# Two DMA lanes and new prices in the planner of a decoder trunk, and its decay stores on GpSimd

## The chip, the cores and the metric

One core of a Trainium2 chip. The metric is the device time of one execution in microseconds, as the median of several runs. TensorE does the matmuls, VectorE, ScalarE and GpSimd the work on elements, SyncE issues most of the DMAs; each engine executes its own instructions in the order in which they were written, and waits at an instruction until the semaphores that it needs are there.

## The reference

A decoder trunk of two layers over 1024 positions of width 1024, in float32. Each layer has a token mixer beside a cross-attention of 4 heads into 256 memory tokens, one combined input projection, one output projection over the concatenated heads, and a squared-ReLU MLP of width 4096; both sums go through a layer norm.

```python
for i in range(DEPTH):                       # 2
    if i % N_MIXERS == 0:
        mix, xq = gdn_mixer(x, ...)          # gated DeltaNet, 8 heads of 128
    else:
        mix, xq = s5_mixer(x, ...)           # 64 groups of 64 complex states
    cross = memory_attention(xq, mem, w_kv_mem[i])
    h = jnp.concatenate([mix, cross], axis=-1) @ w_o[i]
    x = layer_norm(DN_ALPHA * x + h, ln1_g[i], ln1_b[i])
    f = jnp.square(jax.nn.relu(x @ mlp_w1[i])) @ mlp_w2[i]
    x = layer_norm(DN_ALPHA * x + f, ln2_g[i], ln2_b[i])
```

In the DeltaNet each head keeps a state S; a chunk of positions is solved with a triangular inverse of a matrix that holds the products of the keys, times beta, times the decay between two positions:

```python
decay = jnp.where(causal, jnp.exp(jnp.where(causal, diff, 0.0)), 0.0)
a_strict = jnp.where(strict, jnp.einsum('bhnid,bhnjd->bhnij', kb, k) * decay, 0.0)
...
attn = jnp.einsum('bhid,bhjd->bhij', qi, ki) * deci
```

## The kernel before, in words

**Matmuls.** A float32 product is made of three matmuls in a format of fewer bits: both operands are split into a high part (a cast by ScalarE) and a low part (the difference, by VectorE), and `mm3` (L422 to L424) adds high·high, low·high and high·low in PSUM. Nearly all of TensorE's time goes there, in steps of 128 by 128 by 512. VectorE's line of such a split is L378, L587, L635 or L991, by what is split.

**The delta rule.** Layer 0 works by head and half of the sequence (a half-head: 512 positions, four tiles of 128). `gdn_keys_out` (L1250) makes for each half-head the decay matrix D (`decay`, L1236: L1241 and L1243), the squared norms of the keys, the scaled keys kd, D times the factors (L1275), and stores D in DRAM (`ded`, L1276, by ScalarE's queue). From the products of the keys (kk, L1282) and D comes NT (L1283); its diagonal blocks go out by four DMAs `ntd` of GpSimd (L1286) and the whole by one, `ntf` (L1287). `gdn_inverse` and `gdn_invert_tiles` read them back and make the inverse in small products (iv, tv, mz: L1403 to L1433; the matmul L1408). `gdn_queries_out` (L1436) turns the queries (qt, L1444), takes their norms on ScalarE (jk, L1446), and reads D back as Dq (L1450, SyncE). `gdn_recur` (L1534) runs over the tiles of a head: ks = S·k (L1554), R (L1556, VectorE), pe = inverse·R (L1560), e (L1562, ScalarE), po (L1557 and L1572), pS (L1566), the next S (L1569 or L1571, VectorE). Projections of the next head (wi, wz, with the convolution at L1218 to L1226) are the work that lies between.

**The S5 layer.** `s5_read` (L2093) adds to each half's output py a product with s5t (L2100) and one of r with H (L2101). H is a tile of 256 KB that GpSimd's queue loads from DRAM (L2035).

**What sets the order.** The code writes the steps down in some order, and at the end of `run` one call of `settle` (L63; called in L2418) puts the instructions of all five engines from the start of layer 0 on into an order of its own. It is a list scheduler: it keeps a model time for each engine, gives each instruction a cost from `price` (L305: busy time, time until the result is there, and for a DMA the time that its bytes take), knows the buffers of each pool, and takes again and again the instruction that can begin first. All DMAs share one server in the model (`served`): each begins to move when the one before has moved. TensorE's order follows the written one within a reach of 40 us, the others may run up to 70 us ahead of what is due. The order that it finds is nailed down by dependencies. So a price changes no instruction, and yet may move any of them.

**The end.** The last layer norm (`layer_norm` with `last`, L550 to L557) works on three pieces of a row of 1024: 512, 256, 256, as the last matmuls deliver them; each piece is scaled in one pass (L554), and a second pass (L556) is followed by the store of that piece.

## Time and profile before

| what | us |
|---|---|
| median of 3 runs | 2468.33 (2463.03 to 2469.39) |
| the profiled execution | 2469.93 |
| its span, first to last instruction | 2468.2 |
| TensorE busy (granted clock 0.998) | 2438.1 |
| VectorE, ScalarE, GpSimd busy | 1928.6, 1302.2, 411.1 |

A row of a timeline gives the start, the duration, engine, line, operation, output and inputs with shapes, the number of instructions in the row, and in brackets how long the engine stood idle before it and what ended that. A matmul is pipelined: its duration overlaps the next one's, and the step from start to start is what it costs. A row of the waits gives who waited for whom: total, times, longest. Names of buffers in the profile lack their numbers; in the order below they have them.

### The profile page before, as it was taken

What the parts mean: (1) busy time and instruction counts of PE and PEld (TensorE: products, weight loads), DVE (VectorE), ACT (ScalarE), POOL (GpSimd) and SP (SyncE); (2) the same over time, 40 slices, a digit from 0 to 9 for tenths busy, and PEclk for the clock granted to TensorE, in tenths of its full rate; (3) what the DMA queues carried; (4) which work ended last, traced back from release to release, by engine and by line L of the source; (5) the groups of instructions that cost most, each with busy time, mean ns of one, the idle gap of its engine ahead of it and who ended that gap; (6) DMA issues with size and microseconds to landing.
All of it is one profiled execution on the core that took longest, in us unless ns stands there. A gap on an engine that the chain in (4) does not pass through costs nothing.

```text
span 2468.2 us, 36630 instructions
## 1 busy us (share of the span) xinstructions
PE 2438.1 (99%) x12055; PEld 2024.0 (82%) x12055; DVE 1928.6 (78%) x3537; ACT 1302.2 (53%) x2779; POOL 411.1 (17%) x629
## 2 busy tenths in 40 slices
PE   9999999999999999999999999999999999999998
PEld 7888888888887887878888888888888888888887
DVE  8786878777779999897888767786688756676868
ACT  7665565555467576554444255464376555544442
POOL 1242333313001034111100133012010000000002
PEclk9999999999999999999999999999999999999999
DMA  6463555747955767787543499569746544666432
GB/s 228 112 178 115 137 164 137 221 131 214 319 198 201 281 223 241 252 289 235 175 152 123 149 273 314 161 226 326 259 138 226 185 152 157 247 190 225 120 120 82
DMA packets 326544, 485.88 MB, mean 197 GB/s; under 512 B 106273, under 2 KB 136945, under 8 KB 326353
## 3 DMA queue, kind: packets, MB, share of 16 engines
q1 hardware_dynamic: 299680, 427.90, 52.9%
q0 software_dynamic: 23936, 50.85, 7.1%
q10 hardware_dynamic: 2736, 4.79, 0.5%
q8 instruction: 95, 1.56, 0.3%
q14 instruction: 97, 0.79, 0.1%
HBM read 325.59 MB, written 157.78 MB: 196 GB/s over the span
## 4 chain that ended last, share of the span: by engine, by line
PE 74%; DVE 9%; issue 7%; DMA 5%; ACT 3%; POOL 2%; SPq 0%; DVEq 0%; ACTq 0%; POOLq 0%
PE q L422 7%; PE q L423 7%; PE q L424 7%; PE tm L423 3%; PE tm L424 3%; PE tm L422 3%; PE pA L422 3%; PE pA L423 3%; PE pA L424 3%; PE wi L422 2%; PE wi L423 2%; PE wi L424 2%; PE pC L422 2%; PE pC L423 2%; PE pC L424 2%
## 5 line engine op out<-in xcount | busy, mean ns | idle before, releaser
L423 PE MATMUL q<-wkl,hkh 128*128 128x512 f32 x784 | 305.7, 390 | 1.1 <-DVE wkl L991 1.1
L422 PE MATMUL q<-wkh,hkh 128*128 128x512 f32 x784 | 305.9, 390 | 0.0
L424 PE MATMUL q<-wkh,hkl 128*128 128x512 f32 x784 | 305.4, 389 | 0.0
L990 ACT CAST wkh<-wr 128x512 fp32r<-128x512 f32 x168 | 105.0, 625 | 243.7 <-PE q L423 238.2
L991 DVE TENSOR_TENSOR wkl<-wr,wkh 128x512 fp32r<-128x512 f32 x168 | 115.9, 690 | 110.2 <-issue 79.3
L423 PEld LDWEIGHTS q<-wkl,hkh 128*128 128x128 f32 x784 | 147.2, 188 | 32.2 <-DVE wkl L991 1.9
L422 PEld LDWEIGHTS q<-wkh,hkh 128*128 128x128 f32 x784 | 147.2, 188 | 31.5 <-ACT wkh L990 0.8
L424 PEld LDWEIGHTS q<-wkh,hkl 128*128 128x128 f32 x784 | 147.2, 188 | 30.5
L549 POOL TENSOR_TENSOR mv<-mv,mhalf 128x1 f32<-128x1 f32 x32 | 29.2, 911 | 844.0 <-DVE mv L543 563.0
L422 PE MATMUL wi<-xTh,wih 128*128 128x512 f32 x384 | 159.2, 415 | 0.3 <-ACT xTh L1097 0.2
L423 PE MATMUL wi<-xTl,wih 128*128 128x512 f32 x384 | 153.1, 399 | 0.9 <-DVE xTl L1098 0.9
L424 PE MATMUL wi<-xTh,wil 128*128 128x512 f32 x384 | 152.8, 398 | 0.0
L991 DVE TENSOR_TENSOR hkl<-hr,hkh 128x512 fp32r<-128x512 f32 x188 | 128.9, 686 | 0.0
L990 ACT CAST hkh<-hr 128x512 fp32r<-128x512 f32 x188 | 116.4, 619 | 0.0
L422 PE MATMUL tm<-so 128*128 128x512 f32 x280 | 110.2, 398 | 0.9 <-ACT so L1746 0.9
L1747 DVE TENSOR_TENSOR so<-or,so 128x1024 fp32r<-128x1024 f32 x70 | 84.5, 1222 | 28.4 <-ACT so L1746 28.1
L1746 ACT CAST so<-or 128x1024 fp32r<-128x1024 f32 x70 | 71.8, 1050 | 58.0 <-DMA or<-wod 40.3
L423 PE MATMUL tm<-so 128*128 128x512 f32 x224 | 87.5, 394 | 0.0
L424 PE MATMUL tm<-so 128*128 128x512 f32 x224 | 87.1, 392 | 0.0
L424 PEld LDWEIGHTS wi<-xTh,wil 128*128 128x128 f32 x384 | 72.3, 188 | 15.0 <-issue 0.8
L422 PEld LDWEIGHTS wi<-xTh,wih 128*128 128x128 f32 x384 | 72.5, 189 | 14.1 <-issue 1.4
L423 PEld LDWEIGHTS wi<-xTl,wih 128*128 128x128 f32 x384 | 72.6, 189 | 12.8 <-DVE xTl L1098 1.6
(626 smaller groups left out, 7256.3 us busy)
## 6 DMA issues: line engine op xcount, KB each, us to landing
hr<-hd SPq DMA_DIRECT2D x204, 256.0 KB, 2.7
wr<-in_w_dram SPq DMA_DIRECT2D x112, 256.0 KB, 5.2
hd<-u SPq DMA_DIRECT2D x92, 256.0 KB, 2.6
w1r<-in_w_dram SPq DMA_DIRECT2D x36, 512.0 KB, 3.6
hd<-hid SPq DMA_DIRECT2D x60, 256.0 KB, 2.3
hd<-p SPq DMA_DIRECT2D x60, 256.0 KB, 2.6
w1r<-in_w_dram SPq DMA_DIRECT2D x56, 256.0 KB, 4.0
wir<-in_w_in_dram SPq DMA_DIRECT2D x23, 512.0 KB, 4.1
```

The source lines that it names most:

```text
L422: mm(ps, a[0], b[0], start=start, stop=False, skip_group_check=onto)
L423: mm(ps, a[0], b[1], start=False, stop=False, skip_group_check=onto)
L424: mm(ps, a[1], b[0], start=False, stop=stop, skip_group_check=onto)
L549: nc.gpsimd.tensor_tensor(mv[:, 3:4], mv[:, 2:3], self.mhalf[:, 0:1], op=ALU.pow)
L990: nc.scalar.copy(hi, s)
L991: nc.vector.tensor_tensor(lo, s, f32(hi), op=ALU.subtract)
L1746: nc.scalar.copy(hi, r)
L1747: V.tensor_tensor(lo, r, f32(hi), op=ALU.subtract)
```

## The change

The change has four parts.

1. The planner's DMA model has two lanes: one for the queues of SyncE and ScalarE, one for GpSimd's. Each has its own server. Where both have work, the new method `carry` makes each slower by half of what overlaps. A lane holds at most eight transfers; the next waits for the eighth before it. What GpSimd issues takes 0.8 us more.
2. `price` has other numbers: for the issue of a DMA (ScalarE 0.3, the others 0.4, GpSimd by the number of pieces), for its latency, for large DMAs of GpSimd, for ScalarE's copies of fewer than 128 partitions and its accumulating reads, for GpSimd's smallest operation and VectorE's small ones.
3. The second pass of the last layer norm runs over two pieces of 512, so there are two stores and not three.
4. The store of D, one for each of the sixteen half-heads, is issued by GpSimd.

The instructions stay the same ones otherwise; lines of the changed kernel are 14 higher in most places.

```diff
-            free, locked, served, head, kind = {e: 0.0 for e in names}, 0.0, 0.0, 0, ""
+            lanes = [[], []]
+            free, locked, served, head, kind = {e: 0.0 for e in names}, 0.0, [0.0, 0.0], 0, ""
...
+                        if cost[x][2] and len(lanes[e == E.Pool]) >= 8:
+                            r = max(r, lanes[e == E.Pool][-8] + lag)
...
-                    served = max(served, r + length - moves) + moves
-                    length = served - r + late
+                    length = self.carry(served, e == E.Pool, r + length - moves, moves) - r + late + (0.8 if e == E.Pool else 0)
+                    lanes[e == E.Pool].append(r + length - late - (0.8 if e == E.Pool else 0))
...
+    def carry(self, served, q, at, moves):
+
+        t = max(served[q], at)
+        both = max(0.0, min(served[not q] - t, 2 * moves))
+        served[q] = t + moves + both / 2
+        served[not q] += both / 2
+        return served[q]
...
-            return (0.45 if i.engine != E.Pool else 0.6), 1.6 + size / 300 + (0.0 if k >= 512 else 0.7) + (2 if i.engine == E.Pool else 0.0), moves
+            issue = {E.Activation: 0.3, E.Pool: 0.5 + 0.36 * size / min(k, 2048) * (2 if size > 500 else 1)}.get(i.engine, 0.4)
+            return issue, 1.6 + size / 300 + (0.0 if k >= 512 else 0.4) + (1.2 if i.engine == E.Pool else 0.0), moves
...
-            t = 0.02 + 0.87e-3 * big if i.opcode == "Memset" else 0.5 if big < 2 else 1.0 if big < 8 else 0.17 + 2.1e-3 * big
+            t = 0.02 + 0.87e-3 * big if i.opcode == "Memset" else 0.95 if big < 2 else 1.0 if big < 8 else 0.17 + 2.1e-3 * big
...
-            for c in at:
+            for c in (slice(0, HALF), slice(HALF, 1024)):
                 nc.vector.scalar_tensor_tensor(y[:, c], y[:, c], mv[:, 3:4], gb[1][:, c], op0=ALU.mult, op1=ALU.add)
                 nc.sync.dma_start(last[0][:, c], y[:, c])
...
-        nc.scalar.dma_start(self.ded[h, hf], d)
+        nc.gpsimd.dma_start(self.ded[h, hf], d)
```

How this moves the instructions is shown at three places. The first is on ScalarE, where the decay matrix D_4610 of a half-head is stored while an inverse is made (iv, tv) and a tile of a recurrence ends (e). Before:

```order
L1562 COPY e_4882<-pe_4880 128x128 [waits PE_49]
L1446 ACTIVATE jk,scr_93<-qt_4823 128x128
L1276 DMA ded<-D_4610 128x512 [waits DMAHW0_49,DVE_49]
L1421 COPY tv_1959<-mz_1960 32x4x32 [waits DVE_49]
L1421 COPY tv_1959<-mz_1960 32x4x32
L1446 ACTIVATE jk,scr_93<-qt_4823 128x128 [waits Activation_49]
L1425 COPY iv_4767<-iv_4860 32x4x32 [waits DVE_49]
L1446 ACTIVATE jk,scr_93<-qt_4823 128x128 [waits Activation_49] x2
L1425 COPY iv_4768<-iv_4860 32x4x32 [waits DVE_49]
```

and after:

```order
L1435 COPY tv_1959<-mz_1960 32x4x32 [waits DVE_49]
L1435 COPY tv_1959<-mz_1960 32x4x32
L1439 COPY iv_4767<-iv_4860 32x4x32 [waits DVE_49,PE_49]
L1576 COPY e_4882<-pe_4880 128x128 [waits PE_49]
L1460 ACTIVATE jk,scr_93<-qt_4823 128x128 [waits Activation_49]
L1235 ACTIVATE vT_4651<-wi_4741,scr_93 128x512 [waits DVE_49]
L1439 COPY iv_4768<-iv_4860 32x4x32 [waits DVE_49]
```

The store is gone from ScalarE's row, the two copies tv and the first iv stand ahead of e, and the second iv stands behind one square jk and the evacuation vT. On GpSimd the store stands ahead of the four ntd stores of its half-head.

The second place is TensorE at the turning of a half-head's queries, qt_4713; R_4738 comes from ks_4736, and qT_4458 is the tile that qt turns. Before:

```order
L1282 MATMUL kk_4638<-kT_278 128x128 x4
L423 MATMUL wi_4741<-xTl_12_130,wih_4656 128x512
L424 MATMUL wi_4741<-xTh_11_129,wil_4657 128x512
L1560 MATMUL pe_4754<-R_4738,iv_3635 128x128
L422 MATMUL wi_4741<-xTh_11_129,wih_4656 128x512
L423 MATMUL wi_4741<-xTl_12_130,wih_4656 128x512
L424 MATMUL wi_4741<-xTh_11_129,wil_4657 128x512
L1557 MATMUL po_4735<-S_4682,gb_4173 128x128
L422 MATMUL wi_4741<-xTh_11_129,wih_4656 128x512
L423 MATMUL wi_4741<-xTl_12_130,wih_4656 128x512
L1444 MATMUL qt_4713<-ident,qT_4458 128x128 x4
```

and after:

```order
L1568 MATMUL ks_4736<-S_4682,kT_278 128x128
L1296 MATMUL kk_4638<-kT_278 128x128 x4
L1574 MATMUL pe_4754<-R_4738,iv_3635 128x128
L436 MATMUL wi_4741<-xTh_11_129,wih_4656 128x512
L437 MATMUL wi_4741<-xTl_12_130,wih_4656 128x512
L438 MATMUL wi_4741<-xTh_11_129,wil_4657 128x512
L436 MATMUL wi_4741<-xTh_11_129,wih_4656 128x512
L1458 MATMUL qt_4713<-ident,qT_4458 128x128 x4
```

Before, 20 rows stand between ks_4736 and qt; now only kk, pe and four matmuls of wi do, and po_4735 comes later. VectorE has, for the same instructions, before:

```order
L1571 SCALAR_TENSOR_TENSOR S_4682<-S_4577,scr_93,pS_4680 128x128
L1226 SCALAR_TENSOR_TENSOR qT_4458<-th_4516,qT_4458 128x512
L1268 TENSOR_TENSOR scr_93<-scr_93 128x4
L1223 SCALAR_TENSOR_TENSOR qT_4459<-cv_4460,scr_93,qT_4459 128x512
L1269 TENSOR_TENSOR scr_93<-scr_93 128x4
L1556 SCALAR_TENSOR_TENSOR R_4738<-ks_4736,scr_93,mix_1742 128x128
```

and after:

```order
L392 TENSOR_TENSOR wzl_4848<-wzr_4845,wzh_4847 128x1024
L1281 RECIPROCAL scr_93<-scr_93 128x4
L1570 SCALAR_TENSOR_TENSOR R_4738<-ks_4736,scr_93,mix_1742 128x128
L1282 TENSOR_TENSOR scr_93<-scr_93 128x4
L1289 TENSOR_TENSOR D_4521<-D_4521,scr_93 128x512
L1283 TENSOR_TENSOR scr_93<-scr_93 128x4
L1297 SCALAR_TENSOR_TENSOR NT_4550<-kk_4549,D_4521 128x512
L702 TENSOR_TENSOR ws_4316<-ws_4315,ws_4316 128x512
L1240 SCALAR_TENSOR_TENSOR qT_4458<-th_4516,qT_4458 128x512
```

The last step on qT_4458 stood ahead of R_4738, and now stands behind it, behind the product in D_4521, NT_4550 and a sum of weights (ws).

The third place is TensorE in the S5 read of the other layer, at the product with H. Before, with wq a projection of the cross-attention's queries:

```order
L2100 MATMUL py_15955<-s5t_14549 128x128
L422 MATMUL wq_16035<-xTh_2658_14185,wqh_16031 128x512
L423 MATMUL wq_16035<-xTl_2659_14186,wqh_16031 128x512
L424 MATMUL wq_16035<-xTh_2658_14185,wql_16032 128x512
L422 MATMUL wq_16035<-xTh_2658_14185,wqh_16031 128x512
L423 MATMUL wq_16035<-xTl_2659_14186,wqh_16031 128x512
L424 MATMUL wq_16035<-xTh_2658_14185,wql_16032 128x512
L2101 MATMUL py_15955<-r_15824,H_2929_15876 128x127
```

and after, the last rows ahead of the same product:

```order
L436 MATMUL wq_16035<-xTh_2658_14185,wqh_16031 128x512
L437 MATMUL wq_16035<-xTl_2659_14186,wqh_16031 128x512
L438 MATMUL wq_16035<-xTh_2658_14185,wql_16032 128x512
L436 MATMUL wq_16035<-xTh_2658_14185,wqh_16031 128x512
L437 MATMUL wq_16035<-xTl_2659_14186,wqh_16031 128x512
L438 MATMUL wq_16035<-xTh_2658_14185,wql_16032 128x512
L436 MATMUL wq_16035<-xTh_2658_14185,wqh_16031 128x512
L2115 MATMUL py_15955<-r_15824,H_2929_15876 128x127
L2114 MATMUL py_15955<-s5t_14549 128x128
```

Between the product with s5t and the one with H stand six matmuls of wq before, and sixteen now (the nine ahead of those shown are of the same three kinds).

## The prediction

> **What bounds the kernel now.** The page's head and its first part come first, because they tell how much there is to win.

> ```profile
> span 2468.2 us, 36630 instructions
> PE 2438.1 (99%) x12055; PEld 2024.0 (82%) x12055; DVE 1928.6 (78%) x3537; ACT 1302.2 (53%) x2779; POOL 411.1 (17%) x629
> ```

> TensorE is busy for all but 2468.2 − 2438.1 = 30.1 us. The change leaves the number of matmuls as it is, so only those 30.1 us can shrink, plus whatever new idle time the new order makes. Next is the view of TensorE's waits: line that waited, what it waited for, total, times, longest.

> ```profile
> PE py L2101 <- DMA H<-h1d: 3.1, 1, 3.1
> PE iv L1408 <- ACT iv L1425: 2.5, 2, 2.1
> PE ks L1554 <- DVE S L1569: 1.9, 2, 1.1
> PE pA L423 <- DVE xB L587: 1.2, 1, 1.2
> PE q L423 <- DVE wkl L991: 1.1, 2, 0.6
> PE z L1046 <- DVE z L1043: 1.1, 1, 1.1
> PE po L1557 <- ACT on L1585: 1.1, 2, 0.6
> ...
> PE pA L424 <- DVE a1l L635: 0.9, 1, 0.9
> ```

> No cause is large; the longest single wait is 3.1 us, 0.13% of the span. The row of z is the start of the program, ahead of the planned stretch, and the end is seen in the timeline of the last microseconds (first TensorE's last matmul, then two of VectorE's instructions of the last layer norm):

> ```profile
> 2458.11 0.28 PE L424 MATMUL tm<-w2h,hk 128*128 128x256 f32 x1
> 2462.37 0.75 DVE L556 SCALAR_TENSOR_TENSOR y<-y,mv,gb 128x512 f32<-128x512 f32 x1
> 2463.04 0.87 DVE L554 SCALAR_TENSOR_TENSOR y<-tm,mv,gb 128x256 f32<-128x256 f32 x2
> ```

> From 2458.4 to 2468.2 TensorE has ended: 9.8 us. So 30.1 − 1.1 − 9.8 = about 19 us is all that a better order could take out between start and end. The forecast is therefore a sum of small waits, each read as a race: how long TensorE has work from what releases a chain until it needs the chain's result (counted in the order), and how long the chain takes (from the rows).

> **Term 1, the load of H.** The timeline of TensorE at the longest wait:

> ```profile
> 1552.37 0.39 PE L423 MATMUL wq<-xTl,wqh 128*128 128x512 f32 x1
> 1552.59 0.40 PE L424 MATMUL wq<-xTh,wql 128*128 128x512 f32 x1
> 1556.12 0.77 PE L2101 MATMUL py<-r,H 128*128 128x127 f32 x2 [3.13 <-DMA H<-h1d]
> ```

> Two 128x512 matmuls start 0.22 us apart (0.227 over a longer stretch), though each is shown as 0.39 long. In the order given with the change, six such rows stand between the two py matmuls before and sixteen now; with what moved ahead of the first of them it is twelve more between the step that releases the load and the use of it. 12 × 0.227 = 2.7 of the 3.13 us: **−2.7**. If the load comes just as much later, the gain is nothing; if all of the wait goes, −3.1.

> **Term 2, the store that held ScalarE.** ScalarE's timeline around the second row of the waits, then two rows of the other engines there:

> ```profile
> 430.88 0.67 ACT L1221 ACTIVATE vT<-wi,scr 128x512 f32<-128x512 f32 x1
> 431.65 0.27 ACT L1562 COPY e<-pe 128x128 f32<-128x128 f32 x1
> 431.81 0.28 ACT L1446 ACTIVATE jk<-qt 128x128 bf16<-128x128 f32 x1
> 431.98 0.21 ACT L1446 ACTIVATION_READ_ACCUMULATOR jk<-qt 128x1 f32 x1
> 434.21 0.33 ACTq L1276 DMA_DIRECT2D ded<-D  x1
> 434.57 0.60 ACT L1421 COPY tv<-mz 32x128 f32<-32x128 f32 x2 [2.39 <-DMA bz<-ntf]
> ...
> 436.79 0.26 ACT L1425 COPY iv<-iv 32x128 f32<-32x128 f32 x1
> ```
> ```profile
> 431.00 0.69 DVE L1275 TENSOR_TENSOR D<-D,scr 128x512 f32<-128x512 f32 x1 [0.20 <-ACT D L1243]
> ...
> 437.10 1.10 PE L1408 MATMUL iv<-tv,na 128*128 128x64 f32 x8 [2.08 <-ACT iv L1425]
> ```

> D is ready at 431.69 and ScalarE is free at 432.19, but the store of D is issued at 434.21, and the row behind it names as releaser the DMA bz<-ntf, a load of SyncE. In the order, this store waits for VectorE and for a DMA completion count. So ScalarE's instructions behind it (tv, jk, iv) stood still for 2.02 us, and TensorE's wait for iv is 2.08. After the change no DMA is on ScalarE. What is late next is the chain from pe: e 0.27, one jk 0.38 (431.81 to 432.19), the new vT 0.67, iv 0.26, about 1.6 us and some latency, against nine 128x512 matmuls and one pS, over 2.0 us. I take the whole wait: **−2.1** (at worst −1.5).

> **What the sixteen stores cost GpSimd.** Rows of the tile's view, of GpSimd's lines, and of the DMA view (last column: us from issue to landing):

> ```profile
> L1276 ACTq DMA_DIRECT2D ded<-D x16: 326/326/353, 47.9 to 518.7; - x16
> L1450 SPq DMA_DIRECT2D Dq<-ded x16: 319/400/737, 174.8 to 599.3; - x16
> L1287 POOL DMA_DIRECT2D ntf<-NT x16 | 9.2, 574 | 1.1 <-DMA tv<-t 1.1
> ntf<-NT POOLq DMA_DIRECT2D x16, 256.0 KB, 3.6
> ded<-D ACTq DMA_DIRECT2D x16, 256.0 KB, 2.9
> ```

> ScalarE is freed of 16 × 0.326 = 5.2 us, on an engine that is busy for 53%: nothing by itself. GpSimd gets 16 × 0.574 = 9.2 us, on top of 17%: nothing either, as long as its queue is not late. Behind each moved store stand the four ntd stores and ntf of the same half-head, 0.57 us later where D and NT are ready at once; NT is one 0.65 to 0.69 us VectorE instruction later than D, which covers it. The store lands some 0.7 us later; the first and the last load of it follow 127 and 81 us behind: hidden. If a store were to wait for a count of GpSimd's own queue, ntd and with it the inverse would slip by as much as ScalarE did here, 2 us, once: in the range.

> [...]

> **Term 3, splits of VectorE.** Of the rows above, xB (1.2), wkl (1.1) and a1l (0.9) are TensorE waiting for the low part of an operand. In the new order seven 128x512 matmuls (1.6 us) stand at xB where its product followed at once, and likewise 0.9 to 3.6 us more at the others. All three go: **−3.2**.

> **Term 4, small ones.** Of ks (1.1 and 0.8) the new order adds 0.4 and 0.9 us of work between S and its use, so 1.2 goes; of po 0.3: **−1.5**.

> **Term 5, a new wait at qt.** Here the order moves the other way: qt now comes after ks, four kk, pe and four wi, while VectorE's last step of qT moved behind R. VectorE's rows there, and TensorE's for kk:

> ```profile
> 417.65 0.35 DVE L1556 SCALAR_TENSOR_TENSOR R<-ks,scr,mix 128x128 f32<-128x128 f32 x1
> ...
> 420.12 1.22 DVE L378 TENSOR_TENSOR wzl<-wzr,wzh 128x1024 fp32r<-128x1024 f32 x1
> 421.26 0.68 DVE L1275 TENSOR_TENSOR D<-D,scr 128x512 f32<-128x512 f32 x1
> 421.89 0.06 DVE L1214 MEMSET cv<- 128x3 f32 x1
> 421.98 0.69 DVE L1283 SCALAR_TENSOR_TENSOR NT<-kk,D 128x512 f32<-128x512 f32 x1
> ```
> ```profile
> 419.70 1.16 PE L1282 MATMUL kk<-kT 128*128 128x128 f32 x8
> ```

> From R on VectorE has R 0.35, D 0.68, NT 0.69, then a sum of ws and the step of qT of NT's size, 0.69 each, and small ones: 3.1 to 3.4. TensorE has kk 0.9 (1.16 less the overlap at its end), pe 0.1 and wi 0.9, about 2.0 to 2.2. That is +0.9 at least; with wzl's 1.22 between S and R not hidden, up to +2.6. I take **+2.0**, since wzl now stands right ahead of R and is near the upper end.

> **Term 6, less room elsewhere.** At seven places (evictions of on, so and hid by ScalarE, and r of the S5 read) the new order leaves 0.2 to 0.7 us less work than the chain took. The nearest price is po's row, 1.1 for two; I take half of that each, 7 × 0.3 = **+2.1** (0 to +4).

> **Term 7, what the order doesn't show.** Over 700 matmuls move by more than a microsecond, mostly away from any wait. I take **+1.5**, between −2 and +4.

> **The last layer norm.** One 512-wide instruction (0.75) in place of two 256-wide (0.87 together): −0.1, and the last store is 512 wide and not 256: +0.1 to +0.2. Nothing.

> Sum: −2.7 − 2.1 − 3.2 − 1.5 + 2.0 + 2.1 + 1.5 = −3.9. The profiled execution took 2469.93, 1.7 more than its span, and 1.6 more than the median 2468.33; so 2466.0 for it, and on the median **2464.4**. Differences below 0.3% (7.4 us) are about what a measurement of this kernel can't tell from no change.

> **The rivals.**
> A, the waits of before go and none come: the planner's prices are nearer to the trace, so terms 5 to 7 vanish, and some of the remaining 19 us goes too: −9.5 to −14, 2454.3 to 2458.8. For it: no row of before shows the new waits. Against: two of them are counted in the order.
> B, nothing net: a wait moves to the next chain, 0 to +4, 2468 to 2472. For it: TensorE at 99% and waits that are spread over 20 causes; of the moved stores only one in sixteen was waited for. [...]
> C, slower: the order of VectorE in the delta rule (R ahead of the last step of qT, qt early) is the planner's rule now and not one place. At the fourteen half-heads of the other heads, 2.0 each: +28 − 9.5 = +18.5, 2486.8. It decides from five such places (9.5 / 2.0) and passes 0.3% from nine. Against: qt's other places have more work ahead of them in the order.

> **How the numbers follow.** Forecast (−1 to −8: 2460.3 to 2467.3) 0.52, A 0.22, B 0.18, C 0.08. Faster by over 0.3% (below 2460.9): A and the forecast's lower edge, 0.25; slower (above 2475.7): C without its first places, 0.07; between, 0.68. The range leaves out the lower end of A and all of C: 2456 to 2472.

> **What would show it.** In the new profile: H's wait at py under 0.6; no DMA on ScalarE, and iv under 0.3 there; no xB, wkl or a1l among the waits over 0.5; a wait of qt for qT of 1 to 2.6 near 423; GpSimd 9 us busier. The forecast is wrong if qt or ks show more than four waits over 1 us, if TensorE's busy time changes by more than 3 us, or if the H load lands later by what TensorE gained.

## The result, and the profile after

The changed kernel takes 2454.3 us (median; 2452.73 to 2455.99), against 2468.33 before: a ratio of 0.9948, 95% interval 0.9934 to 0.9962, or 14.0 us less. The forecast was 2464.4 with a range from 2456.0: the measured time lies 1.7 us below its lower end, at the far end of the rival A (the waits of before go and none come). By the ratio the gain is 12.8 us.

The profiled execution after took 2452.73, its head and first part are:

```profile
span 2451.0 us, 36624 instructions
PE 2430.7 (99%) x12055; PEld 2022.4 (83%) x12055; DVE 1932.3 (79%) x3536; ACT 1301.1 (53%) x2779; POOL 419.6 (17%) x645
```

Between the two profiled executions lie 17.2 us of span, 3.2 more than between the medians: the one of before was one of its slower ones, that of after one of its faster ones. GpSimd has sixteen more instructions and 8.5 us more work, as it should. TensorE's busy time is 7.4 us shorter (2438.1 before), and its idle time falls by 9.8, from 30.1 to 20.3. The prediction had named a change of the busy time by more than 3 us as a sign that it is wrong. The view of TensorE's waits, its longest rows:

```profile
PE wi L437 <- DVE xTl L1112: 1.6, 2, 1.3
PE po L1571 <- ACT on L1599: 1.2, 1, 1.2
PE z L1060 <- DVE z L1057: 1.1, 1, 1.1
PE pA L436 <- ACT hid L657: 1.1, 1, 1.1
PE wi L436 <- ACT qT L1235: 0.9, 1, 0.9
PE wq L436 <- DVE ql L1675: 0.8, 1, 0.8
PE pB L436 <- ACT wsh L648: 0.6, 1, 0.6
```

The rows of H, iv, ks, xB and pC are gone, and so is that of q for wkl; that of a1l has 0.5 left of 0.9. The longest wait is 1.3 and not 3.1. All rows of the view add up to 11.1, and to 19.8 before. Where the idle time went is seen in the table of stretches; columns are the stretch, its length, the busy time and instructions of TensorE, of its weight loads, of VectorE, ScalarE and GpSimd, then TensorE's granted clock, the DMA share and GB/s. Of before, then of after, with the boundaries moved along with the work:

```profile
47.00:600.00 553.00, 546.69 (x3097) 457.76 (x3097) 429.63 (x886) 322.21 (x1001) 186.79 (x306) 1.00 0.55 156
600.00:1080.00 480.00, 474.05 (x2226) 387.29 (x2225) 423.06 (x837) 287.58 (x538) 86.28 (x138) 1.00 0.73 251
1080.00:1450.00 370.00, 368.15 (x1794) 305.50 (x1792) 305.63 (x525) 154.54 (x269) 48.34 (x79) 1.00 0.56 180
1450.00:1800.00 350.00, 346.21 (x1751) 294.15 (x1750) 244.46 (x421) 170.28 (x292) 61.54 (x67) 0.99 0.80 256
```
```profile
47.00:600.00 553.00, 549.49 (x3127) 463.04 (x3126) 433.40 (x890) 323.32 (x1006) 197.25 (x322) 1.00 0.55 158
600.00:1080.00 480.00, 477.57 (x2243) 392.00 (x2242) 431.64 (x849) 293.46 (x551) 86.72 (x139) 1.00 0.75 256
1080.00:1440.00 360.00, 359.27 (x1757) 298.89 (x1756) 297.82 (x512) 147.58 (x256) 47.31 (x78) 1.00 0.56 177
1440.00:1790.00 350.00, 348.91 (x1778) 295.30 (x1777) 249.04 (x426) 175.49 (x304) 61.23 (x68) 1.00 0.80 257
```

Idle time falls from 6.3 to 3.5 us in the delta rule, from 6.0 to 2.4 in the stretch that is mostly the MLP of layer 0, from 1.9 to 0.7 and from 3.8 to 1.1 in the last two. It is no one place. The clock column has 0.99 in one row of before: that row hides a cost which the prediction missed, and which the experiments show.

The place of term 2 in ScalarE's timeline of after, without any DMA:

```profile
431.23 0.27 ACT L1576 COPY e<-pe 128x128 f32<-128x128 f32 x1
431.39 0.28 ACT L1460 ACTIVATE jk<-qt 128x128 bf16<-128x128 f32 x1
431.68 0.20 ACT L1460 ACTIVATION_READ_ACCUMULATOR jk<-qt 128x1 f32 x1
431.79 0.67 ACT L1235 ACTIVATE vT<-wi,scr 128x512 f32<-128x512 f32 x1
432.81 0.26 ACT L1439 COPY iv<-iv 32x128 f32<-32x128 f32 x1 [0.35 <-DVE iv L1438]
```

The chain from e to the last iv is as predicted, 1.84 us long (432.81 + 0.26 − 431.23), and no wait of iv is left. At term 5's place TensorE does wait, but ahead of qt and not at it:

```profile
414.66 0.46 PE L1574 MATMUL pe<-R,iv 128*128 128x128 f32 x2 [0.21 <-issue]
416.07 0.50 PE L436 MATMUL wi<-xTh,wih 128*128 128x512 f32 x1 [0.94 <-ACT qT L1235]
...
417.31 0.63 PE L1458 MATMUL qt<-ident,qT 128*128 128x128 f32 x4
```

The 0.94 is a wait for ScalarE, which evacuates the bank that wi needs. By the time that it is over, qT is nearly done.

### The profile page after: what moved, and what is told of

It is laid out like the page before. It is cut to its first block, busy times and chain, and to the rows that moved or that the text cites. A ratio compares the mean times of both kernels' runs of the same rounds, so it can differ in the third digit from the quotient of the medians.

```text
span 2451.0 us, 36624 instructions
## 1 busy us (share of the span) xinstructions
PE 2430.7 (99%) x12055; PEld 2022.4 (83%) x12055; DVE 1932.3 (79%) x3536; ACT 1301.1 (53%) x2779; POOL 419.6 (17%) x645
## 6 DMA issues: line engine op xcount, KB each, us to landing
hr<-hd SPq DMA_DIRECT2D x204, 256.0 KB, 2.7
wr<-in_w_dram SPq DMA_DIRECT2D x112, 256.0 KB, 5.1
hd<-u SPq DMA_DIRECT2D x92, 256.0 KB, 2.3
hd<-hid SPq DMA_DIRECT2D x60, 256.0 KB, 2.5
hd<-p SPq DMA_DIRECT2D x60, 256.0 KB, 2.4
w1r<-in_w_dram SPq DMA_DIRECT2D x56, 256.0 KB, 3.6
```

## The experiments

**Theories.** Theory 1: the new order removed many small waits, and the largest of before, the one for H, cost more than its 3.13 us of idle time, since TensorE's granted clock was low behind it. Its rivals: the engine of the stores carries the gain; or the waits are what single executions make of them. Theories 2 to 4 and the rivals D to I came up on the way, and each stands with the expectation of its run. Each time below is the median of its own runs; "before" ran along on the same chip each time, at 2467.8 to 2469.3.

**Ten matmuls ahead of H.** Edit, behind the planner in before: of the order that it found, only this is changed.

```diff
         order = best[1]
+        at = ...  # the first py product with this H on TensorE
+        more = [x for x in pe[at:at + 80] if name(ins[x].outs[0]) == name(ins[pe[at - 1]].outs[0])][:10]
+        order = [x for x in order if x not in more]
+        k = order.index(pe[at])
+        order[k:k] = more
```

> The order of before, with one edit: the ten matmuls of wq that stood behind the first S5 products with H are put ahead of them (sixteen there and not six), nothing else moves. Theory 1 (the 3.13 us of idle TensorE also lowered its granted clock, so the 28 passes of py behind it took 0.21 us each and not 0.11): the idle time falls to 0.9 us or less, the passes step by 0.11, and the kernel gains 2.3 + 2.8 = about 5 us. Rival 1 (the clock was low there for another cause, such as the 28 plain float32 passes in a row): only the idle time goes, -2.3 us, and the passes still step by 0.21. Rival 2 (the load comes when the queue lets it, and the gap only moves): under 0.5 us.

Measured: 2467.87, ratio 1.0003 (0.9994 to 1.0012). Rival 2 by the time; by the profile the idle time was gone and the passes stepped by 0.11. Both are right, since the wait for H is no fixture of this kernel: the run with the two-piece layer norm, in whose trace TensorE has the same instructions in the same order as in before, had none either, and neither had the run with the stores moved and the order kept. The rows of the first:

```profile
1555.18 0.39 PE L424 MATMUL wq<-xTh,wql 128*128 128x512 f32 x1
1555.41 0.38 PE L2101 MATMUL py<-r,H 128*128 128x127 f32 x2
1555.63 0.39 PE L2100 MATMUL py<-s5t 128*128 128x128 f32 x2
```

So the longest row of the waits that the prediction worked from was one execution's, and by the interval (0.9994) the median of before holds at most 1.5 us of it. As a test of the clock this run told nothing.

**The stores on GpSimd, the order kept.** Before, with the planner made to believe that ScalarE issues them.

```diff
+        ins = [As(i, E.Activation) if i.name in self.moved else i for i in traced[k0:k1]]
...
-        nc.scalar.dma_start(self.ded[h, hf], d)
+        self.moved.add(nc.gpsimd.dma_start(self.ded[h, hf], d).ins.name)
```

> The order of before kept for every instruction, only that the sixteen stores of D are issued by GpSimd at the places where ScalarE had them. Theory (one of sixteen stores kept ScalarE waiting, 2.1 us, and nothing else of the move matters): -2.1 us, the wait of iv near 437 us gone, no other wait over 0.5 us new. Rival A (nothing in the move, the waits turn up elsewhere): within 0.5 us. Rival B (GpSimd's slower issue delays ntd and ntf behind it, and the inverse with them): slower by 1 us or more, with a wait of iv for bz or tv.

Measured: 2462.9, ratio 0.9979 (0.9970 to 0.9987): −5.3 us, more than any of the three had. ScalarE's timeline there, in the same order as before but for the store:

```profile
430.60 0.27 ACT L1571 COPY e<-pe 128x128 f32<-128x128 f32 x1
430.77 0.28 ACT L1455 ACTIVATE jk<-qt 128x128 bf16<-128x128 f32 x1
430.93 0.20 ACT L1455 ACTIVATION_READ_ACCUMULATOR jk<-qt 128x1 f32 x1
431.16 0.60 ACT L1430 COPY tv<-mz 32x128 f32<-32x128 f32 x2
```

tv follows jk at once, where it stood still for 2.39 us before, and TensorE's iv has no wait there. That is the predicted 2.1, shown. A second gain wasn't foreseen: the wait of ks for S at 268 us (1.1) is down to nothing, because a DMA of GpSimd that stood at 259.15 in before is issued at 257.37, and all that follows it on the way to S comes 1.0 us sooner. Why it can be issued sooner isn't shown. These two make 3.2 of the 5.3 us; the rest isn't traced to a place, and new waits came up as well (pC for u 1.5, wi for xTl 1.2).

**The new order, the stores back on ScalarE.** The same device in the changed kernel.

```diff
-        nc.gpsimd.dma_start(self.ded[h, hf], d)
+        self.moved.add(nc.scalar.dma_start(self.ded[h, hf], d).ins.name)
```

> The changed kernel with its whole order kept, only that the sixteen stores of D are issued by ScalarE again, at the places where GpSimd has them. Theory (the new order did it, the store's engine hardly): 0 to +2.5 us against the changed kernel, so 2454 to 2457, still 11 us or more below before. Rival (the engine of the stores carries the gain): +8 us or more, 2462 or above.

Measured: 2454.99 (ratio to before 0.9947, 0.9935 to 0.9959): 0.7 above the changed kernel, and by the ratios no different from it. The theory held and its rival fell. In the new order the stores' engine is worth next to nothing, in the old one 5 us: the two parts of the change cover for each other.

**The last layer norm alone.**

```diff
-            for c in at:
+            for c in (slice(0, HALF), slice(HALF, 1024)):
```

> Before with the last layer norm's second pass in two pieces and two stores, no other instruction moved. Theory of the prediction: within 0.3 us of before. The two traces of before and after differ by 0.95 us from the last matmul to the end; if the two pieces are the cause of that, -0.9 us, seen in the profile between TensorE's end and the end of the span.

Measured: 2468.32, ratio 1.0003 (0.9995 to 1.0012). The median can't tell 0.9 from nothing; the profile can. From TensorE's last start to the end of the span it is 2468.2 − 2458.11 = 10.1 before and 2466.3 − 2457.11 = 9.2 here:

```profile
2460.46 1.53 DVE L554 SCALAR_TENSOR_TENSOR y<-tm,mv,gb 128x512 f32<-128x512 f32 x3
2461.91 1.40 DVE L556 SCALAR_TENSOR_TENSOR y<-y,mv,gb 128x512 f32<-128x512 f32 x2
```

The three scalings now all run ahead of the second pass (before, the first piece's second pass stood between them), and the last store starts the sooner. The prediction had put this at nothing.

**Half of the planner.** Each with the stores on GpSimd: the two lanes, `carry` and the prices of DMAs alone; the prices of the engines' operations alone; and neither, so that the old planner plans around the moved stores. The edits are the hunks of the change, chosen.

> Of the change only the planner's DMA model (two lanes, carry, eight in a lane, the new prices of DMAs) and the stores on GpSimd; the old prices of engine operations, the old last layer norm. Measured by itself, the move of the stores in the old order gave 2462.9; the whole change 2454.3. Theory 2 (the 8 us between come from the 600 to 1180 us stretch, where waits for VectorE and ScalarE were removed by both halves of the new prices): 2457 to 2460. Rival D (the DMA model carries it): 2456 or less. Rival E (the engine prices carry it): 2461 to 2464.

> The counterpart: only the new prices of ScalarE's, GpSimd's and VectorE's small operations and the stores on GpSimd; the old DMA model. Theory 2: 2457 to 2460. Rival D: 2461 to 2464. Rival E: 2456 or less.

> Before with the one line changed that issues the stores from GpSimd, so that the old planner plans around them anew. Theory 2 (the store's move takes away the block on ScalarE and no more): as with the order kept, 2461 to 2464. Rival F (the replanned order is as arbitrary as any and moves the time by itself): outside 2460 to 2466.

Measured: 2463.69 (0.9979, 0.9970 to 0.9989), 2462.01 (0.9974, 0.9963 to 0.9984) and 2457.92 (0.9955, 0.9938 to 0.9971). Theory 2 fell, and so did D and E, since neither half is below 2461: each half is slower than neither by the medians, though the intervals overlap a little. And the old planner's two orders with the same stores, 2462.9 kept and 2457.9 replanned, differ by 5 us (rival F), with intervals that just touch. A single order is a draw with several microseconds of spread.

**How wide the draw is.** The planner's constants changed by a little, in before and in the changed kernel.

```diff
-        self.settle(self.begin, ..., reach=40.0, ahead=70.0, margin=0.2, late=0.7)
+        self.settle(self.begin, ..., reach=40.0, ahead=70.0, margin=0.25, late=0.7)
...
+        self.settle(self.begin, ..., reach=40.0, ahead=70.0, margin=0.2, late=0.8)
```

> Before, with one constant of its planner changed (the margin that it adds ahead of TensorE 0.25 us and not 0.20): another order by the same model, none of the change in it. Theory 3 (the new planner's model is better, the single order matters less): 2463 to 2471. Rival G (any order of either planner is a draw from the same spread of small waits): anywhere from 2454 to 2470.

> Before, with another constant changed (lateness of DMAs 0.8 us and not 0.7). Theory 3: 2463 to 2471. Rival G: anywhere from 2454 to 2470.

> The changed kernel with the margin 0.25 us and not 0.20. Theory 3: 2452 to 2459, below every order of the old planner. Rival G: anywhere from 2454 to 2470, overlapping with the old planner's two.

> The changed kernel with the lateness of DMAs 0.8 us and not 0.7. Theory 3: 2452 to 2459. Rival G: anywhere from 2454 to 2470.

Measured: 2466.10 (0.9998, 0.9988 to 1.0008), 2462.24 (0.9976, 0.9966 to 0.9985), 2458.75 (0.9965, 0.9951 to 0.9978) and 2452.25 (0.9940, 0.9924 to 0.9957). Theory 3 missed the second, by 0.8 us. Then the new planner with the stores left on ScalarE and planned there (every hunk but the last two), and the same two constants for the old planner with the stores on GpSimd:

> The new planner (DMA model and all prices), planning with the stores of D on ScalarE; the old last layer norm. The fourth corner beside before (2468.3), the old planner with the stores on GpSimd (2457.9) and the whole change (2454.3). Theory 3 (the new planner plans around the store wherever it is): 2452 to 2459. Rival H (the block of ScalarE by a store's completion count comes back and the planner can't see it): 2459 to 2466, with a wait of iv or ks of 1 us or more behind a store on ScalarE.

> The old planner with the stores of D on GpSimd, and its margin 0.25 us and not 0.20. So far: old planner, stores on ScalarE 2468.3, 2466.1, 2462.2 (three orders); old planner, stores on GpSimd 2457.9 (replanned) and 2462.9 (order kept); new planner 2454.3, 2458.8, 2452.3 and 2456.9. Theory 4 (store and planner each give a few us on the mean of the orders, and one order lies up to 5 us from the mean): 2458 to 2464, the mean of the orders with old planner and GpSimd between the two other groups, near 2461. Rival I (the old planner does as well as the new one once the stores are on GpSimd): 2452 to 2457.

> The same with the lateness of DMAs 0.8 us and not 0.7, the margin 0.20. Theory 4: 2458 to 2464. Rival I: 2452 to 2457.

Measured: 2456.92 (0.9957, 0.9940 to 0.9974), 2460.99 (0.9959, 0.9944 to 0.9974) and 2459.83 (0.9953, 0.9937 to 0.9970). Rival H fell by the time, and the longest wait of iv there, 1.1 us, stands behind a load and not behind a store. Together:

| planner's constants | old planner, ScalarE | old planner, GpSimd | new planner, GpSimd |
|---|---|---|---|
| margin 0.20, late 0.7 | 2468.3 (before) | 2457.9 | 2454.3 (after) |
| margin 0.25, late 0.7 | 2466.1 | 2461.0 | 2458.8 |
| margin 0.20, late 0.8 | 2462.2 | 2459.8 | 2452.3 |
| mean | 2465.5 | 2459.6 | 2455.1 |

In each row the stores' move takes time off (10.4, 5.1, 2.4) and the new planner, which has the new last layer norm with it, takes off some more (3.6, 2.2, 7.6, from unrounded medians). On the means of these medians that is −5.9 and −4.5, as theory 4 had it, and the first and third columns don't overlap, against rival G. Of the 14.0 us, 10.4 would belong to the change by these means; 2.8 are that before is the slowest order of its three, and 0.8 that after lies below the mean of its own.

The second step is weaker than it looks. By the ratios to the before that ran beside each, the means of the columns are 0.9991, 0.9956 and 0.9951: 8.8 us for the stores and 1.2 for the planner, 0.9 of which is the layer norm by its profile. Each ratio is known to about 0.0015 (3.7 us), so rival I, that the old planner does as well once the stores are on GpSimd, is not excluded. Nor does the split say what each part is worth by itself: with the stores left on ScalarE the new planner has 0.9957, and the old one with the stores on GpSimd 0.9955. In one order each, either part alone gives most of the gain. The kernel with lateness 0.8 in the new planner is the fastest found: 2452.25 (2451.85 to 2452.84), ratio to before 0.9940 (0.9924 to 0.9957), 2 us below the changed kernel, though the two weren't timed side by side.

**What a long wait costs.** The clock behind idle TensorE, from seven of these profiles, none of which was made for it. The stretches of before behind the wait for H (the third number from the end is the granted clock), and the rows of the same stretch of the kernel with two pieces, where the wait wasn't there:

```profile
1556.00:1558.00 2.00, 1.88 (x9) 1.91 (x10) 0.41 (x1) 0.00 (x0) 0.00 (x0) 0.50 1.03 188
1558.00:1560.00 2.00, 2.00 (x11) 2.00 (x11) 0.86 (x3) 0.51 (x1) 0.00 (x0) 0.50 0.36 119
1560.00:1562.00 2.00, 2.00 (x11) 2.00 (x11) 0.00 (x0) 0.09 (x1) 0.00 (x0) 0.50 0.57 158
```
```profile
1556.00:1558.00 2.00, 2.00 (x21) 2.00 (x20) 1.93 (x4) 0.60 (x1) 0.00 (x0) 1.00 1.06 179
```

Half the clock for 6 us: nine matmul records in 2 us and not twenty-one. The two products with H and s5t step by 0.43 there and by 0.22 in the other run, fourteen times, which makes 2.9 us on top of the 3.1. The same happened elsewhere in other executions: in the kernel with two pieces after a wait of iv, and in the replanned kernel with the stores on GpSimd after a wait for a cast (so), where single 128x512 matmuls start 0.43 us apart for 3.4 us:

```profile
437.74 1.11 PE L1408 MATMUL iv<-tv,na 128*128 128x64 f32 x8 [2.69 <-ACT iv L1425]
```
```profile
439.00:440.00 1.00, 1.00 (x6) 0.80 (x5) 0.77 (x4) 0.25 (x1) 0.86 (x2) 0.51 0.95 318
440.00:441.00 1.00, 1.00 (x4) 0.75 (x3) 1.00 (x2) 0.57 (x2) 1.00 (x3) 0.50 0.99 269
```
```profile
1742.01 0.65 PE L422 MATMUL tm<-so 128*128 128x512 f32 x1 [2.91 <-ACT so L1746]
1742.46 0.63 PE L423 MATMUL tm<-so 128*128 128x512 f32 x1
1742.89 0.63 PE L424 MATMUL tm<-so 128*128 128x512 f32 x1
```

The length of the wait does not decide it. Behind 1.80 us in the old planner's order with the stores on GpSimd and the margin 0.25, behind 1.71 in the run with the prices of the engines' operations alone, and behind 2.23 in the run with the new planner and the stores on ScalarE, the clock was halved:

```profile
917.83 0.50 PE L422 MATMUL pC<-xB,s1h 128*128 128x512 f32 x1 [1.80 <-ACT s1h L634]
918.30:921.60 3.30, 3.30 (x9) 2.39 (x8) 3.30 (x8) 2.19 (x5) 2.06 (x4) 0.50 0.88 282
```
```profile
1082.85 0.49 PE L424 MATMUL q<-wkh,hkh 128*128 128x512 f32 x1 [1.71 <-ACT wkh L992]
1083.70:1087.00 3.30, 3.17 (x8) 2.51 (x9) 3.30 (x7) 2.74 (x6) 0.94 (x2) 0.50 0.93 290
```
```profile
918.42 0.50 PE L438 MATMUL pA<-xB,a1l 128*128 128x512 f32 x1 [2.23 <-DVE a1l L649]
919.70:923.00 3.30, 3.30 (x9) 2.58 (x8) 3.13 (x7) 2.57 (x5) 1.86 (x4) 0.50 0.51 181
```

Behind the 2.08 us wait of iv in before, and behind 2.34 in the kernel with ten matmuls moved, it stayed at 1.00 (from 436 to 443 us in before; of the other, these rows):

```profile
437.25 1.10 PE L1415 MATMUL iv<-tv,na 128*128 128x64 f32 x8 [2.34 <-ACT iv L1432]
438.00:440.00 2.00, 2.00 (x17) 1.73 (x15) 1.78 (x6) 1.03 (x3) 1.35 (x3) 1.00 0.89 279
```

Part of the difference of the medians is of this kind too. Of the 81 executions of before beside the experiments, the 10 with a mean granted clock of 0.999 have a median of 2465.3 us, the 46 with 0.998 one of 2468.1, and the 23 with 0.997 one of 2470.1; all five of the changed kernel have 0.999. The waits themselves are in these differences, so how much of them is the clock stays open.

## Why the prediction was wrong, point by point

**What held.** TensorE is the bound, at 99% on both sides, and what it waited for shrank. Term 2 was right in mechanism, and its size was measured by itself at the place: the block of 2.0 us on ScalarE went with the store. GpSimd's share was hidden: a store takes 0.60 us of it, and the first and the last are read 125 and 77 us later:

```profile
L1290 POOL DMA_DIRECT2D ded<-D x16: 551/604/767, 48.4 to 515.3; - x16
L1464 SPq DMA_DIRECT2D Dq<-ded x16: 319/382/599, 173.7 to 591.9; - x16
```

**What failed.** Two steps did. The first is "only those 30.1 us can shrink": of the 17.2 us between the profiles 7.4 came out of TensorE's busy time, and no term of the sum looked there. The second is the losses of terms 5 to 7: +5.6 in the sum, and +1.7 in the view.

- *The gains.* The prediction named 9.5 us of waits as gone, and the rows that it named (H, iv, ks, xB, wkl, a1l) fall by 10.4. All rows together fall by 8.7, so the others grew by 1.7. By the starts of TensorE's instructions the fall is about 11.1, because a wait cost more than the idle time beside it: iv's row shows 2.08, and from the start of the matmul ahead of it (434.63) to its own (437.10) it is 2.47, of which a step is 0.23, so 2.24. About 0.17 for each wait, in terms 1 to 4 left out.
- *Term 1* was 2.7 and in the profiled execution 6.0 with the clock, but on the median it was worth at most 1.5, since other executions of the same order had no such wait. Both errors come from reading one execution: a wait that ends with a DMA's landing is a sample. Other waits of the same order varied too: pC for u 0.8, 1.7 and 2.6 in all in three profiles, tm for so at 1.7 ms none in one and 1.6 us in another.
- *Term 5* was 0.21 + 0.94 = 1.15 at the place, against 2.0, and at another instruction than forecast.
- *Term 6*, +2.1, named the right kind (po 1.2 and 0.6, hid 1.1, so 0.2: 3.1 after), but waits of that kind went as well (po 1.1, so 0.9, hid 0.2: 2.2 before), so +0.9 is left.
- *Term 7*, +1.5 for what the order doesn't show, had no row behind it and the wrong sign: the rows of the view that no other term names hardly changed (6.7 before, 6.4 after), and the small steps outside the view fell by 2.3.
- *The last layer norm* was worth −0.9 in the profile and not nothing, too little for the median to show: the second pass of the first piece had stood between the scalings.

Of the profiles' 17.2 us, about 11.1 are waits by the starts, 2.9 the clock behind H, 0.9 the end; 2.3 are small steps that no row names. The time is that of rival A at its lower end, and this is luck: A said that no new waits come, and they did (po 1.2, hid 1.1, qT 0.9, ql 0.8), while the clock, the end and the draw of the order, which A doesn't name, made up for them. Rival C (qt in all half-heads) fell: no qt wait is in the view. What stays open is which of the planner's prices matters, since each half alone gave nothing beyond the stores' move, and whether the new planner is worth anything beside that move: more than three orders a group would have to tell.

## What to carry to other kernels

When a scheduler's prices change, the new order is a draw as much as an improvement: time two or three neighbouring settings of its constants on both sides before the difference is put down to the model, and compare each with the old kernel that ran beside it. Read waits that end with a DMA from more than one execution, and price a wait by the starts around it, with the clock behind it: here it was halved behind waits of 1.71 to 3.13 us, though not behind those of 2.08 and 2.34. A store on ScalarE's queue held that engine here for 2.02 us, by the profile until a load of SyncE had landed; where the stores' readers are far off (77 to 125 us here), an otherwise idle engine (GpSimd, busy for 17%) is the place for them.

## What the runs showed of the hardware

How soon the store of 256 KB lands hangs on the order as much as on its queue. The rows of the changed kernel, with ntf, from which the prediction took its 0.7, and the row of the run with the new order and the stores back on ScalarE:

```profile
ded<-D POOLq DMA_DIRECT2D x16, 256.0 KB, 2.7
ntf<-NT POOLq DMA_DIRECT2D x16, 256.0 KB, 3.5
```
```profile
ded<-D ACTq DMA_DIRECT2D x16, 256.0 KB, 2.3
```

In the new order that is 2.7 us after the issue from GpSimd's queue and 2.3 from ScalarE's; in the old order it was 2.9 from ScalarE's. So the order made 0.6 us on one queue, and the queue 0.4 in one order. The issue cost 0.60 us of GpSimd and not the 0.33 that it had cost of ScalarE. And behind a wait of TensorE of 1.71 us its granted clock was 0.50 for 3.3 us and more, where behind one of 2.34 us it stayed at 1.00; what decides between them is not shown.
